# Gate rows of a two-layer streaming encoder: from weighted row sums to row sums of turned weights with a round trip through DRAM, and seven raw buffers in place of four

## The chip, the core and the metric

The kernel runs on one core of one Trainium2 chip. The metric is the device time of one execution in microseconds (us). TensorE is called PE, VectorE DVE, ScalarE ACT, GpSimd POOL, and SyncE SP; SP here only issues transfers (DMAs).

## What is computed

There are 256 tokens of 2048 features and two layers. In each layer a conditioning vector `c` gives six vectors of 2048 numbers (shift, scale and gate for the mixers, and the same three for the feed-forward part). This is the part that the change touches:

```python
c_act = jax.nn.silu(c)
for l in range(DEPTH):
    mod = (c_act @ w_mod[l] + b_mod[l]).reshape(bn, 6, d)
    ...
    h = layer_norm(x) * (1.0 + scale_m) + shift_m
    proj = h @ w_in[l]
    ...            # four groups of mixers, 512 columns each, give y
    y = jnp.concatenate([y_a, y_b, y_c, y_d], axis=-1) @ w_out[l]
    x = layer_norm(ALPHA * x + (1.0 + gate_m) * y, post_mix_g[l], post_mix_b[l])
    h = layer_norm(x) * (1.0 + scale_f) + shift_f
    y = conv_ffn(h, ffn_w_up[l], ffn_w_conv[l], ffn_b_conv[l], ffn_w_down[l])
    x = layer_norm(ALPHA * x + (1.0 + gate_f) * y, post_ffn_g[l], post_ffn_b[l])
```

All data are float32. `w_mod` is the largest part: 2048 x 12288 numbers in each layer, so 16 MB for each of the six vectors.

## The kernel before

**Products.** Weights come from DRAM in pieces of 1 MB into a buffer of the pool `rawp` (128 partitions x 2048 floats, four buffers; `weights`, line 368). ACT copies a piece into a rounded half `whi` (line 397), DVE takes the difference `wlo` (line 398), and PE multiplies `whi` and `wlo` with the two halves of the activations (`mm`, line 94). Both halves live in `splitp`, four buffers each. Where activations or weights are taken exactly (the first pieces of layer 0, the six first units of the second half of its output projection, the first group behind each norm), weights go straight into `splitp` or `slotp` buffers as `wexact` (line 381), without ACT and DVE.

**Order of the parts.** Layer 0 takes its mixers by pieces (`by_pieces`, line 1181), because its first shift and scale are themselves still being computed: units of modulation, conv block D and side groups U, V, E, B follow a list of turns. Then come group C, the attention, the output projection `out_proj` (line 603, tile `o`), the FFN up (tiles `g_c`, `v_c`), the FFN down (`out_proj` again, tile `d`), and layer 1 in the same way with whole groups. `out_proj` makes the 2048 output columns in two halves. When the last unit of the first half is reached it asks for the gate (line 762), and `finish_bank` multiplies each result bank with it (line 641, tile `yg`). Six PSUM buffers hold the results; a half takes four.

**Modulation.** It runs beside the products, on DVE. `mod_stream` (line 290) lists its parts, and `pump` takes some steps of it for each unit of weights, at rates written by hand for each phase (`RATES`, line 35). `need` (line 320) takes the steps that are missing when a vector is asked for. Each step loads 1 MB of `w_mod` into a raw buffer, so modulation and weights share the four buffers. Shift and scale are wanted as columns (one number for each partition): the weights lie turned in DRAM (`w_mod_turned`), and one instruction multiplies 128 rows of 2048 with `silu(c)` broadcast over the partitions (`cB`) and adds up each row (`row_sum`, line 191).

**Gates before.** A gate is wanted as a row that stands on all partitions. `gate_steps` (line 274) loads 16 pieces of `w_mod_gates` and adds them, each times one column of `silu(c)`, to `macc` (128 x 2048, a buffer of its own; `mod_step`, line 222). After the 16th the bias row is loaded into a raw buffer (`brow`, line 283) and added on partition 0 (line 286). The sum is then put into the list `late`. `settle` runs `gate_rows` (line 230) on it: the sum is split into halves `mhi` and `mlo` (lines 417 and 418, in `splitp` buffers), eight products with a matrix of ones sum over the partitions and spread the result (`ps_gate`), and four ACT copies add 1 and write the row `gate` (line 239). `settle` is called two steps into the next part, at the start of the next gate, or by `need`; for the last gate (layer 1, FFN) no part follows, so `need` calls it.

**Who orders the instructions.** The framework (Tile) fixes each engine's order when the program is built: it walks the program with a model of the engines, gives buffers out as they come free, and lets a free engine take the earliest written instruction whose inputs and buffers are there. So an instruction that is written late can be issued early where its engine has nothing older to do. SP and POOL issue their DMAs in that order, and an issue that waits for its buffer holds what stands behind it. A few order edges are written by hand (`held`, line 351: eight splits and six modulation steps wait for a norm).

POOL issues the small parameter loads (`load_params`, line 178) and makes the reciprocal roots of the norms (`power`, line 124).

Of the kernel before, what the change touches and what calls it, by code (L numbers as in the profile page):

```python
# [7 lines left out]
F32 = mybir.dt.float32  # L8
F32R = mybir.dt.float32r
AF = mybir.ActivationFunctionType  # L10
ALU = mybir.AluOpType
AX = mybir.AxisListType

P = 128
D = 2048
S = 256
DEPTH = 2
W_G = 512
KT = D // P
# [12 lines left out]
SHIFT_M, SCALE_M, GATE_M, SHIFT_F, SCALE_F, GATE_F = range(6)  # L32
# [16 lines left out]
LATE_KT = 12  # L49
# [2 lines left out]

LEAD, UNIT_LEAD = 2, 4

PAIRS = ((SHIFT_M, SCALE_M), (SHIFT_F, SCALE_F))

GROUPS = {
    "w_in": ((C_UV, 512), (C_UV + 512, 512), (C_Q, 768), (C_SB, 512), (C_SC, 1024), (C_AG, 1024)),
    "w_out": ((0, 1024), (1024, 1024)),
# [6 lines left out]
def encoder_kernel(ctx: ExitStack, tc: tile.TileContext, A: dict, consts: bass.AP, out: bass.AP):  # L66
    nc = tc.nc
    pe, act, dve, pool = nc.tensor, nc.scalar, nc.vector, nc.gpsimd

    keep = ctx.enter_context(tc.tile_pool(name="keep", bufs=1))  # L70
    rawp = ctx.enter_context(tc.tile_pool(name="rawp", bufs=4))
    splitp = ctx.enter_context(tc.tile_pool(name="splitp", bufs=4))
    tmpp = ctx.enter_context(tc.tile_pool(name="tmpp", bufs=4))
    actp = ctx.enter_context(tc.tile_pool(name="actp", bufs=10))
    slotp = ctx.enter_context(tc.tile_pool(name="slotp", bufs=11))
    smallp = ctx.enter_context(tc.tile_pool(name="smallp", bufs=2))
    accp = ctx.enter_context(tc.tile_pool(name="accp", bufs=6, space=bass.MemoryType.PSUM))
    msp = ctx.enter_context(tc.tile_pool(name="msp", bufs=2, space=bass.MemoryType.PSUM))


    def raw_tile(name):
        return rawp.tile([P, 2048], F32, tag="raw", name=name)

    def tmp_tile(name):
        return tmpp.tile([P, 512], F32, tag="tmp", name=name)

    def ms_tile(name):
        return msp.tile([P, 512], F32, tag="ms", name=name)
# [4 lines left out]
    def mm(o, lhsT, rhs, start, stop):  # L93
        pe.matmul(o, lhsT, rhs, start=start, stop=stop, skip_group_check=True)  # L94

    def ident_act(o, i, scale, bias):
        return act.activation(out=o, in_=i, func=AF.Identity, scale=scale, bias=bias)
# [7 lines left out]
    ident = cst[:, 0:128]  # L105
# [2 lines left out]
    rotdup = cst[0:64, 384:512]  # L108
    cosT = cst[:, 512:768]
    sinT = cst[:, 768:1024]  # L110
    flat = tmp_tile("flat")
    pool.memset(flat[:, 0:P], 1.0)
    pool.memset(flat[:, P : P + 16], 0.0)
    for j in range(4):
        pool.memset(flat[:, P + 5 * j : P + 5 * j + 1], 1.0)
    onesR = keep.tile([P, P + 16], F32R, name="onesR")
    act.copy(onesR, flat[:, : P + 16])
    ones = onesR[:, 0:P].bitcast(F32)
    mhalf = keep.tile([P, 4], F32, name="mhalf")
    pool.memset(mhalf, -0.5)  # L120
    eps = keep.tile([P, 1], F32, name="eps")
# [23 lines left out]
    bcol = []  # L145
# [3 lines left out]
    pool.dma_start(out=bcol[0], in_=A["b_mod_cols"][0])  # L149

    def scales_up(l):
        b = bcol[l].rearrange("p (h m) -> p h m", h=2)[:, :, KT : 2 * KT]
        dve.tensor_scalar(out=b, in0=b, scalar1=1.0, scalar2=None, op0=ALU.add)

    scales_up(0)
# [40 lines left out]

    def mod_unit(l, m, kt, total):
        raw = raw_tile("wmod")
        pair = PAIRS.index((m, m + 1)) if m in (SHIFT_M, SHIFT_F) else PAIRS.index((m - 1, m))
        nc.sync.dma_start(out=raw, in_=A["w_mod_turned"][l, 2 * pair + m % 3, kt])  # L200
        row_sum(raw, D, 0, total)

    def mod_done(l, m, k0, n, total):
# [9 lines left out]
                MOD[(l, m + h, k0 + k)] = cols[:, h, k : k + 1]  # L213
        return i

    def halves(acc, c0, width=1024):
        hi = splitp.tile([P, 1024], F32R, tag="whi", name="mhi")[:, :width]
        lo = splitp.tile([P, 1024], F32R, tag="wlo", name="mlo")[:, :width]
        split((hi, lo), acc[:, c0 : c0 + width])
        return [(hi[:, i : i + 512], lo[:, i : i + 512]) for i in range(0, width, 512)]  # L220

    def mod_step(acc, w, kt, first):
        col = cact[:, kt : kt + 1]
        if first:
            i = dve.tensor_scalar(out=acc, in0=w, scalar1=col, scalar2=None, op0=ALU.mult)
        else:
            i = dve.scalar_tensor_tensor(out=acc, in0=w, scalar=col, in1=acc, op0=ALU.mult, op1=ALU.add)  # L227
        held(i, "mod")

    def gate_rows(l, m, acc):  # L230

        g = keep.tile([P, D], F32, tag="gate", name=f"gate_{l}_{m}")
        for h in range(2):
            for i, (hi, lo) in enumerate(halves(acc, h * 1024)):
                c0 = h * 1024 + i * 512
                ps = ms_tile("ps_gate")
                mm(ps, onesR[:, 0:P], hi, True, False)
                mm(ps, onesR[:, 0:P], lo, False, True)
                ident_act(g[:, c0 : c0 + 512], ps, 1.0, ones[:, 0:1])
        GATE[(l, m)] = g  # L240

    GATE = {}
# [7 lines left out]
    def load_late_first():  # L250
        for m in (SHIFT_F, SCALE_F):
            for h in range(2):
                half = slot("wlate")
                nc.sync.dma_start(out=half, in_=A["w_mod_turned"][0, 2 + m % 3, LATE_KT, :, h * 1024 : (h + 1) * 1024])
                late_first[(m, h)] = half

    def columns(l, m, k0, k1):
# [16 lines left out]
    def gate_steps(l, m):  # L274
        while late:
            settle()
        acc = tmpp.tile([P, D], F32, tag="macc", name="macc", bufs=1)
        for kt in range(KT):
            raw = raw_tile("wmod")
            nc.sync.dma_start(out=raw, in_=A["w_mod_gates"][l, m // 3, kt])  # L280
            if kt == KT - 1:
                row = raw_tile("brow")
                nc.sync.dma_start(out=row[0:1, :], in_=A["b_mod"][l : l + 1, m * D : (m + 1) * D])
            mod_step(acc, raw, kt, kt == 0)
            if kt == KT - 1:
                dve.tensor_tensor(out=acc[0:1, :], in0=acc[0:1, :], in1=row[0:1, :], op=ALU.add)
                late.append((l, m, acc))
            yield

    def mod_stream():  # L290
# [60 lines left out]
    def held(i, kind):  # L351

        name, n = hold[kind]
        if n > 0:
            hold[kind][1] = n - 1
            tc.add_manual_dep(i.ins, name, order_dep, reason="the norm is what the next products wait for")
# [58 lines left out]
    def split(dst, src):  # L415
        hi, lo = dst[:2]
        i = act.copy(hi, src)
        dve.tensor_tensor(out=lo, in0=src, in1=hi.bitcast(F32), op=ALU.subtract)
        return i
# [1104 lines left out]


_INS = [
    "x", "b_mod", "gmlp_ln_g", "gmlp_ln_b", "gmlp_b_s", "mla_w_ukv", "post_mix_g", "post_mix_b",
    "post_ffn_g", "post_ffn_b",
]

# [1 line left out]
def _laid_out(inputs):  # L1532

    import numpy as np

    get = lambda name: np.asarray(inputs[name])
    cols = lambda name: get(name).reshape(DEPTH, -1, P).transpose(0, 2, 1)
    arrays = {name: get(name) for name in _INS}
    for name, groups in GROUPS.items():
        w = get(name)  # L1540
        for c0, width in groups:
            per = 2048 // width
            part = w[:, :, c0 : c0 + width].reshape(DEPTH, -1, per, P, width)
            arrays[f"{name}_{c0}_{width}"] = part.transpose(0, 1, 3, 2, 4)
    w = get("w_mod").reshape(DEPTH, D, 2, 3, KT, P)
    arrays["w_mod_turned"] = w[:, :, :, :2].transpose(0, 2, 3, 4, 5, 1).reshape(DEPTH, 4, KT, P, D)
    arrays["w_mod_gates"] = w[:, :, :, 2].transpose(0, 2, 1, 3, 4).reshape(DEPTH, 2, KT, P, D)
    arrays["c_cols"] = get("c").reshape(KT, P).T
    arrays["b_mod_cols"] = cols("b_mod")
    arrays["mixer_cols"] = np.concatenate(  # L1550
        [
            cols(name)
            for name in ("conf_w_dw", "mla_q_norm", "mla_kv_norm", "sconv_w", "conf_b_dw", "conf_ln_g", "conf_ln_b")
        ],
        axis=2,
    )
    arrays["ffn_cols"] = np.concatenate([cols("ffn_w_conv"), cols("ffn_b_conv")], axis=2)
    arrays["gmlp_w_turned"] = get("gmlp_w_s").transpose(0, 3, 1, 2).reshape(DEPTH, P, -1)
    uq = get("mla_w_uq").reshape(DEPTH, 3, P, HEADS, 192)
    arrays["mla_w_uq"] = np.concatenate(  # L1560
        [uq[..., :128].reshape(DEPTH, 3, P, -1), uq[..., 128:].reshape(DEPTH, 3, P, -1)], axis=3
    )
    return {name: np.ascontiguousarray(a) for name, a in arrays.items()}
# [28 lines left out]
def build(inputs):  # L1592
    import numpy as np
    import concourse.bacc as bacc

    nc = bacc.Bacc("TRN2", target_bir_lowering=False, num_devices=1)
    arrays, A = {}, {}
    for name, a in _laid_out(inputs).items():
        arrays[f"in_{name}_dram"] = a
        A[name] = nc.dram_tensor(f"in_{name}_dram", a.shape, mybir.dt.from_np(a.dtype), kind="ExternalInput").ap()  # L1600
    c = _constants()
    arrays["in_consts_dram"] = c
    consts = nc.dram_tensor("in_consts_dram", c.shape, F32, kind="ExternalInput").ap()
    out = nc.dram_tensor("out_0_dram", (1, S, D), F32, kind="ExternalOutput").ap()
    with tile.TileContext(nc) as tc:
        encoder_kernel(tc, A, consts, out)
    return nc, arrays
# [8 lines left out]
```

## Time and profile before

| what | value |
|---|---|
| median of 3 runs | 2243.66 us (2242.68 to 2244.53) |
| the profiled execution's own time | 2246.46 us |
| its span (first to last instruction) | 2244.7 us |
| mean granted clock of PE | 0.991 |
| data moved by DMA | 605.17 MB |

The profile shows one execution. A page gives the busy time of each engine, the chain of work that ended last, and the costliest groups of instructions; other views give the waits, the instructions in order of time, one tile's instructions, or a table by stretches of time. "Idle before, releaser" says how long an engine waited and for whom. Matmuls overlap: a busy PE is not yet a PE at its peak, and the distance from the start of one matmul to that of the next is what it costs.

### The profile page before, as it was taken

To read this page: it belongs to the slowest core of one execution; us is meant where nothing else is said; L and a number is where in the kernel's file an instruction comes from. 1 tells how busy PE (TensorE), PEld (TensorE's weight loads), DVE (VectorE), ACT (ScalarE), POOL (GpSimd) and SP (SyncE) were. 2 spreads that over 40 slices of the span, in tenths; PEclk is the share of its full clock that TensorE was granted. 3 is DMA by queue.
4 is the path that set the end of the run, shared out by engine and by line. 5 is a ranking of instruction groups with operands and counts; after the bars stand their busy time and mean duration, and the time that the engine had idled before them with its cause. 6 is when DMAs were issued, how large, how long until landed. Compare 5 with 4: busy or idle time off the path is not lost.

```text
span 2244.7 us, 30821 instructions
## 1 busy us (share of the span) xinstructions
PE 2200.6 (98%) x12128; PEld 1901.5 (85%) x12128; DVE 1738.9 (77%) x2222; ACT 1067.3 (48%) x1579; POOL 29.6 (1%) x49
## 2 busy tenths in 40 slices
PE   7999999999999999999999999999999999999997
PEld 5788885898888888888889899888888888888886
DVE  6778986988888888989876998977775656575756
ACT  3457541454455445544444435445444544454542
POOL 0000000000000000000000000000000000000000
PEclk9999999999999999999999999999999999999999
DMA  9999689688888888888867666865665555555553
GB/s 390 350 390 386 239 340 359 247 308 315 313 316 308 329 318 320 328 330 322 336 219 263 209 232 252 305 224 208 245 224 192 184 199 179 203 189 188 187 194 144
DMA packets 94235, 605.17 MB, mean 270 GB/s; under 512 B 10660, under 2 KB 10852, under 8 KB 28932
## 3 DMA queue, kind: packets, MB, share of 16 engines
q1 hardware_dynamic: 93752, 602.29, 71.8%
q8 instruction: 95, 1.56, 0.3%
q0 software_dynamic: 336, 0.89, 0.1%
q14 instruction: 52, 0.43, 0.1%
HBM read 601.05 MB, written 2.10 MB: 269 GB/s over the span
## 4 chain that ended last, share of the span: by engine, by line
PE 80%; DVE 4%; DMA 1%; ACT 1%; issue 1%; POOL 0%; DVEq 0%; ACTq 0%; POOLq 0%
PE g_c L94 23%; PE v_c L94 22%; PE d L94 21%; PE o L94 5%; PE C_c L94 2%; PE D_c L94 2%; PE U_c L94 1%; PE B_c L94 1%; PE E_c L94 1%; DVE wlo L398 1%; DMA wraw<-in_w_out_dram 1%; DVE convD L827 1%; PE ps_xT L534 0%; DVE wmod L192 0%; DMA wmod<-in_w_mod_turned_dram 0%
## 5 line engine op out<-in xcount | busy, mean ns | idle before, releaser
L397 ACT CAST whi<-wraw 128x1024 fp32r<-128x1024 f32 (+1 forms) x632 | 647.9, 1045 | 873.2 <-PE g_c L94 208.1
L398 DVE TENSOR_TENSOR wlo<-wraw,whi 128x1024 fp32r<-128x1024 f32 (+1 forms) x632 | 752.9, 1214 | 307.6 <-ACT whi L397 290.0
L94 PE MATMUL d<-whi,a 128*128 128x512 f32 x1344 | 364.1, 389 | 0.0
L94 PE MATMUL v_c<-hT,whi 128*128 128x512 f32 (+1 forms) x1456 | 341.8, 383 | 0.0
L94 PE MATMUL g_c<-hT,whi 128*128 128x512 f32 (+1 forms) x1344 | 313.3, 380 | 0.0
L192 DVE SCALAR_TENSOR_TENSOR wmod<-wmod,cB 128x2048 f32<-128x2048 f32 x126 | 287.4, 2286 | 31.9 <-DMA wmod<-in_w_mod_turned_dram 31.6
L94 PEld LDWEIGHTS v_c<-hT,whi 128*128 128x128 f32 x1456 | 264.5, 189 | 48.2 <-DVE g L1388 0.3
L94 PEld LDWEIGHTS d<-whi,a 128*128 128x128 f32 x1344 | 252.2, 188 | 52.5 <-ACT whi L397 0.2
L94 PEld LDWEIGHTS g_c<-hT,whi 128*128 128x128 f32 x1344 | 243.4, 189 | 43.2
L94 PE MATMUL d<-wlo,a 128*128 128x512 f32 x672 | 209.9, 389 | 0.0
L94 PE MATMUL v_c<-hT,wlo 128*128 128x256 f32 x1400 | 190.2, 283 | 0.0
L94 PEld LDWEIGHTS v_c<-hT,wlo 128*128 128x128 f32 x1400 | 183.1, 191 | 6.5
L94 PE MATMUL g_c<-hT,wlo 128*128 128x256 f32 x1280 | 175.8, 283 | 0.0
L94 PEld LDWEIGHTS g_c<-hT,wlo 128*128 128x128 f32 x1280 | 168.2, 191 | 5.9
L227 DVE SCALAR_TENSOR_TENSOR macc<-wmod,cact,macc 128x2048 f32<-128x2048 f32 x60 | 140.7, 2345 | 17.3 <-DMA wmod<-in_w_mod_gates_dram 17.2
L94 PEld LDWEIGHTS d<-wlo,a 128*128 128x128 f32 x672 | 126.2, 188 | 26.2
L94 PE MATMUL o<-whi,a 128*128 128x512 f32 x384 | 109.7, 395 | 2.4 <-ACT whi L397 2.4
L94 PEld LDWEIGHTS o<-whi,a 128*128 128x128 f32 x384 | 71.8, 188 | 20.1 <-ACT whi L397 4.1
L94 PE MATMUL D_c<-hT,whi 128*128 128x256 f32 x432 | 81.6, 292 | 1.7 <-ACT whi L397 1.7
L1337 DVE SCALAR_TENSOR_TENSOR u<-g,pf,u 128x254 f32<-128x254 f32 (+1 forms) x176 | 73.3, 476 | 0.0
L94 PEld LDWEIGHTS D_c<-hT,whi 128*128 128x128 f32 x432 | 68.8, 197 | 4.4 <-ACT whi L397 2.8
L94 PE MATMUL o<-wlo,a 128*128 128x512 f32 x192 | 63.0, 397 | 0.6 <-DVE wlo L398 0.5
(343 smaller groups left out, 2505.4 us busy)
## 6 DMA issues: line engine op xcount, KB each, us to landing
wraw<-in_ffn_w_up_dram SPq DMA_DIRECT2D x168, 1024.0 KB, 4.9
wmod<-in_w_mod_turned_dram SPq DMA_DIRECT2D x126, 1024.0 KB, 6.3
wraw<-in_ffn_w_down_dram SPq DMA_DIRECT2D x88, 1024.0 KB, 4.8
wmod<-in_w_mod_gates_dram SPq DMA_DIRECT2D x64, 1024.0 KB, 5.0
wraw<-in_w_in_dram SPq DMA_DIRECT2D x27, 1024.0 KB, 5.5
wraw<-in_w_out_dram SPq DMA_DIRECT2D x26, 1024.0 KB, 5.8
wexact<-in_w_in_dram SPq DMA_DIRECT2D x46, 512.0 KB, 9.6
wexact<-in_ffn_w_up_dram SPq DMA_DIRECT2D x16, 512.0 KB, 9.5
```

The source lines that it names most:

```text
L94: pe.matmul(o, lhsT, rhs, start=start, stop=stop, skip_group_check=True)
L192: i = dve.scalar_tensor_tensor(out=raw, in0=raw, scalar=1.0, in1=cB[:, k0 : k0 + n], op0=ALU.mult, op1=ALU.mult, accum_out=total)
L227: i = dve.scalar_tensor_tensor(out=acc, in0=w, scalar=col, in1=acc, op0=ALU.mult, op1=ALU.add)
L397: cast[0] = act.copy(hi[:, :m], r)
L398: i = dve.tensor_tensor(out=lo[:, :m], in0=r, in1=hi[:, :m].bitcast(F32), op=ALU.subtract)
L827: dve.scalar_tensor_tensor(out=yd[:, j, 30 - k :], in0=glu[:, j, : S - 30 + k], scalar=CW(k, j), in1=yd[:, j, 30 - k :], op0=ALU.mult, op1 ...
L1337: dve.scalar_tensor_tensor(out=u[:, sh:], in0=x[:, : S - sh], scalar=col(k, j), in1=u[:, sh:], op0=ALU.mult, op1=ALU.add)
```

## The change

The gates are now computed like shift and scale. `gate_steps` takes 16 row sums of turned weights into `total` (128 x 16), adds the bias columns (to which `scales_up` now adds the 1 as well), and puts the 128 x 16 result into `late`. `gate_rows` turns it with one PE transposition, copies the 16 x 128 result out of PSUM on ACT, writes it to DRAM as a row of 2048 (a POOL DMA of 8 KB), and loads that row back onto all 128 partitions (a second POOL DMA of 1 MB, which waits for the first). `macc`, `brow`, the splits, the eight products and the four copies go. The weights of all six vectors lie in `w_mod_turned`. The matrix of ones is set by one DVE instruction where POOL and ACT made it before.

The raw pool has seven buffers of 8 KB per partition where it had four. The space comes from `macc` (8 KB) and from the descriptor space of POOL's DMAs, which is set to 2048 bytes per partition (16384 when nothing is said).

```diff
-    rawp = ctx.enter_context(tc.tile_pool(name="rawp", bufs=4))
+    rawp = ctx.enter_context(tc.tile_pool(name="rawp", bufs=7))
...
+    dramp = ctx.enter_context(tc.tile_pool(name="dramp", bufs=1, space=bass.MemoryType.DRAM))
...
-    flat = tmp_tile("flat")
-    pool.memset(flat[:, 0:P], 1.0)
...
-    onesR = keep.tile([P, P + 16], F32R, name="onesR")
-    act.copy(onesR, flat[:, : P + 16])
-    ones = onesR[:, 0:P].bitcast(F32)
+    onesR = keep.tile([P, P], F32R, name="onesR")
+    dve.memset(onesR.bitcast(F32), 1.0)
+    ones = onesR.bitcast(F32)
...
-        b = bcol[l].rearrange("p (h m) -> p h m", h=2)[:, :, KT : 2 * KT]
+        b = bcol[l].rearrange("p (h m) -> p h m", h=2)[:, :, KT : 3 * KT]
...
-        pair = PAIRS.index((m, m + 1)) if m in (SHIFT_M, SHIFT_F) else PAIRS.index((m - 1, m))
-        nc.sync.dma_start(out=raw, in_=A["w_mod_turned"][l, 2 * pair + m % 3, kt])
+        nc.sync.dma_start(out=raw, in_=A["w_mod_turned"][l, m, kt])
         row_sum(raw, D, 0, total)
...
-    def gate_rows(l, m, acc):
-
+    def gate_rows(l, m, cols):
+
+        ps = ms_tile("ps_gate")
+        pe.transpose(ps[0:KT, 0:P], cols, ident)
+        rows = tmp_tile("grows")[0:KT, 0:P]
+        act.copy(rows, ps[0:KT, 0:P])
+        flat = dramp.tile([KT, P], F32, tag=f"gate{l}{m}", name=f"gate_row_{l}_{m}")
+        pool.dma_start(out=flat, in_=rows)
         g = keep.tile([P, D], F32, tag="gate", name=f"gate_{l}_{m}")
-        for h in range(2):
-            for i, (hi, lo) in enumerate(halves(acc, h * 1024)):
-                c0 = h * 1024 + i * 512
-                ps = ms_tile("ps_gate")
-                mm(ps, onesR[:, 0:P], hi, True, False)
-                mm(ps, onesR[:, 0:P], lo, False, True)
-                ident_act(g[:, c0 : c0 + 512], ps, 1.0, ones[:, 0:1])
+        pool.dma_start(out=g, in_=flat.rearrange("k j -> (k j)").partition_broadcast(P))
         GATE[(l, m)] = g
...
-        acc = tmpp.tile([P, D], F32, tag="macc", name="macc", bufs=1)
+        total = smallp.tile([P, KT], F32, tag="gtotal", name="gtotal", bufs=1)
         for kt in range(KT):
-            raw = raw_tile("wmod")
-            nc.sync.dma_start(out=raw, in_=A["w_mod_gates"][l, m // 3, kt])
+            mod_unit(l, m, kt, total[:, kt : kt + 1])
             if kt == KT - 1:
-                row = raw_tile("brow")
-                nc.sync.dma_start(out=row[0:1, :], in_=A["b_mod"][l : l + 1, m * D : (m + 1) * D])
-            mod_step(acc, raw, kt, kt == 0)
-            if kt == KT - 1:
-                dve.tensor_tensor(out=acc[0:1, :], in0=acc[0:1, :], in1=row[0:1, :], op=ALU.add)
-                late.append((l, m, acc))
+                cols = smallp.tile([P, KT], F32, tag="gcols", name="gcols", bufs=1)
+                dve.tensor_tensor(out=cols, in0=total, in1=bcol[l][:, m * KT : (m + 1) * KT], op=ALU.add)
+                late.append((l, m, cols))
             yield
...
-    nc = bacc.Bacc("TRN2", target_bir_lowering=False, num_devices=1)
+    nc = bacc.Bacc("TRN2", target_bir_lowering=False, num_devices=1, dynamic_dma_scratch_size=2048)
```

More of the change, by code (lines that the diff above doesn't have):

```diff
@@ L53 @@
 LEAD, UNIT_LEAD = 2, 4
-PAIRS = ((SHIFT_M, SCALE_M), (SHIFT_F, SCALE_F))
 GROUPS = {
@@ L110, in encoder_kernel @@
     sinT = cst[:, 768:1024]
-    flat = tmp_tile("flat")
-    pool.memset(flat[:, 0:P], 1.0)
-    pool.memset(flat[:, P : P + 16], 0.0)
-    for j in range(4):
-        pool.memset(flat[:, P + 5 * j : P + 5 * j + 1], 1.0)
-    onesR = keep.tile([P, P + 16], F32R, name="onesR")
-    act.copy(onesR, flat[:, : P + 16])
-    ones = onesR[:, 0:P].bitcast(F32)
+    onesR = keep.tile([P, P], F32R, name="onesR")
+    dve.memset(onesR.bitcast(F32), 1.0)
+    ones = onesR.bitcast(F32)
     mhalf = keep.tile([P, 4], F32, name="mhalf")
@@ L214, in mod_done @@
         return i
[L216 to L228, printed above, removed]
-    def gate_rows(l, m, acc):
-        g = keep.tile([P, D], F32, tag="gate", name=f"gate_{l}_{m}")
-        for h in range(2):
-            for i, (hi, lo) in enumerate(halves(acc, h * 1024)):
-                c0 = h * 1024 + i * 512
-                ps = ms_tile("ps_gate")
-                mm(ps, onesR[:, 0:P], hi, True, False)
-                mm(ps, onesR[:, 0:P], lo, False, True)
-                ident_act(g[:, c0 : c0 + 512], ps, 1.0, ones[:, 0:1])
+    def gate_rows(l, m, cols):
[5 more added lines that the diff above has]
+        pool.dma_start(out=flat, in_=rows)
+        g = keep.tile([P, D], F32, tag="gate", name=f"gate_{l}_{m}")
+        pool.dma_start(out=g, in_=flat.rearrange("k j -> (k j)").partition_broadcast(P))
         GATE[(l, m)] = g
@@ L253, in load_late_first @@
                 half = slot("wlate")
-                nc.sync.dma_start(out=half, in_=A["w_mod_turned"][0, 2 + m % 3, LATE_KT, :, h * 1024 : (h + 1) * 1024])
+                nc.sync.dma_start(out=half, in_=A["w_mod_turned"][0, m, LATE_KT, :, h * 1024 : (h + 1) * 1024])
                 late_first[(m, h)] = half
@@ L1526 @@
 _INS = [
-    "x", "b_mod", "gmlp_ln_g", "gmlp_ln_b", "gmlp_b_s", "mla_w_ukv", "post_mix_g", "post_mix_b",
+    "x", "gmlp_ln_g", "gmlp_ln_b", "gmlp_b_s", "mla_w_ukv", "post_mix_g", "post_mix_b",
     "post_ffn_g", "post_ffn_b",
@@ L1544, in _laid_out @@
             arrays[f"{name}_{c0}_{width}"] = part.transpose(0, 1, 3, 2, 4)
-    w = get("w_mod").reshape(DEPTH, D, 2, 3, KT, P)
-    arrays["w_mod_turned"] = w[:, :, :, :2].transpose(0, 2, 3, 4, 5, 1).reshape(DEPTH, 4, KT, P, D)
-    arrays["w_mod_gates"] = w[:, :, :, 2].transpose(0, 2, 1, 3, 4).reshape(DEPTH, 2, KT, P, D)
+    w = get("w_mod").reshape(DEPTH, D, 6, KT, P)
+    arrays["w_mod_turned"] = w.transpose(0, 2, 3, 4, 1)
     arrays["c_cols"] = get("c").reshape(KT, P).T
```

## The prediction

> **What bounds the kernel now.** I read the head of the page first, then the chain of work that ended last in order of time, and then the busy times by stretches. On the page:
>
> ```profile
> span 2244.7 us, 30821 instructions
> ...
> PE 2200.6 (98%) x12128; PEld 1901.5 (85%) x12128; DVE 1738.9 (77%) x2222; ACT 1067.3 (48%) x1579; POOL 29.6 (1%) x49
> ...
> PE 80%; DVE 4%; DMA 1%; ACT 1%; issue 1%; POOL 0%; DVEq 0%; ACTq 0%; POOLq 0%
> ```
>
> PE is busy nearly all the time and makes 80% of the chain. So an edit pays in two ways only: it takes work off PE where PE runs without a break, or it shortens one of the places where PE waits. The table by stretches (columns: length, then PE, PEld, DVE, ACT, POOL busy with counts, PE clock, DMA share, GB/s) tells which stretch is which. First the three that hold the gates 2 to 4 (layer 0 FFN, layer 1 mixer, layer 1 FFN):
>
> ```profile
> 600.00:650.00 50.00, 50.00 (x288) 43.86 (x288) 43.29 (x53) 28.58 (x44) 0.00 (x0) 1.00 0.83 322
> ...
> 1350.00:1400.00 50.00, 49.99 (x398) 48.91 (x396) 44.44 (x57) 26.41 (x34) 0.00 (x0) 1.00 0.67 244
> ...
> 2100.00:2150.00 50.00, 50.00 (x221) 40.90 (x220) 36.42 (x41) 26.98 (x33) 0.00 (x0) 1.00 0.51 180
> ```
>
> PE has no break in them, at full clock, while DVE and DMA have room: here a matmul less is time less. Then layer 0's mixer, in which gate 1 lies, in finer steps:
>
> ```profile
> 10.00:20.00 10.00, 4.16 (x13) 1.91 (x11) 8.68 (x17) 5.70 (x11) 3.15 (x2) 0.75 1.02 419
> ...
> 50.00:60.00 10.00, 10.00 (x44) 7.47 (x43) 2.10 (x6) 4.46 (x8) 0.00 (x0) 1.00 0.72 291
> 60.00:70.00 10.00, 9.76 (x64) 8.58 (x63) 8.94 (x10) 6.59 (x13) 0.00 (x0) 1.00 0.81 304
> 70.00:80.00 10.00, 7.86 (x43) 6.67 (x43) 9.39 (x14) 3.86 (x8) 0.00 (x0) 0.99 0.91 338
> 80.00:90.00 10.00, 9.26 (x50) 9.07 (x51) 7.80 (x10) 2.84 (x5) 0.00 (x0) 0.67 1.00 362
> ...
> 260.00:270.00 10.00, 10.00 (x50) 8.81 (x49) 9.24 (x14) 2.13 (x5) 0.00 (x0) 1.00 0.29 107
> ...
> 310.00:320.00 10.00, 10.00 (x45) 8.21 (x45) 10.00 (x11) 4.38 (x7) 0.00 (x0) 1.00 0.77 307
> ...
> 330.00:340.00 10.00, 9.14 (x37) 6.27 (x36) 7.95 (x8) 4.00 (x4) 0.00 (x0) 1.00 1.01 384
> 340.00:350.00 10.00, 8.09 (x35) 6.05 (x34) 9.47 (x9) 1.99 (x2) 0.00 (x0) 1.00 0.99 363
> ```
>
> PE waits at 70 to 90 and at 330 to 350, and after the first wait its clock falls to 0.67 for ten microseconds. Yet DMA, which reaches 419 GB/s, ran at 291 and 304 just before the first wait, and at 107 some way before the second. What stops it is told by SP's own waits over the first 420 us, and what PE waited for by the instructions around 77 us:
>
> ```profile
> SPq L200 <- DVE wlo L398: 57.9, 17, 13.7
> SPq L386 <- DVE wmod L192: 41.6, 14, 9.8
> ```
>
> ```profile
> 77.47 1.04 ACT L397 CAST whi<-wraw 128x1024 fp32r<-128x1024 f32 x1 [3.44 <-DMA wraw<-in_w_in_dram]
> ...
> 78.56 0.97 PE L94 MATMUL D_c<-hT,whi 128*128 128x256 f32 x6 [1.69 <-ACT whi L397]
> ```
>
> Modulation loads (L200) wait until a weight piece is split, and weight loads (L386) until a modulation piece is summed: the two take turns in four buffers, 99.5 us of waiting in these two rows alone. When the buffer comes, the piece lands late, ACT waits 3.44 us for it and PE 1.69 us for ACT.
>
> **The change, part by part. 1: gate products off PE.** The chain around gate 2 (start, length, what):
>
> ```profile
> 602.14 22.27 PE g_c L94 x128
> 624.87 0.68 PE v_c L94 x3
> 626.21 1.37 PE v_c L94 x6
> 628.27 0.70 PE ps_gate L94 x3
> 628.98 19.75 PE v_c L94 x117
> 648.72 22.27 PE g_c L94 x128
> ...
> 1389.98 0.93 PE ps_gate L94 x4
> ...
> 1496.47 3.57 PE g_c L94 x32
> ```
>
> A group of 128 matmuls takes 22.27 us. The group that holds the gate starts at 602.14 + 22.27 = 624.41 and ends at 648.72, 24.31 us: the gate costs 2.04 us (its eight matmuls at 0.70 / 3 = 0.23 us are 1.87 of them). In its place comes one transposition, 128 columns wide. The last row is 32 exact matmuls of that width, 0.11 us each. So a gate gives 1.93 us, and the three in stretches without a break give **5.8 us**. Gate 1's products also go, 1.87 - 0.11 = **1.8 us**, but PE waits 60 us later, at 330 to 350: this counts only if those waits shrink too, so I count it with the buffers.
>
> **2: DVE and ACT.** Work around one gate, by tile (ns min/median/max):
>
> ```profile
> L227 DVE SCALAR_TENSOR_TENSOR macc<-wmod,cact,macc x60: 2322/2346/2353, 162.7 to 1648.3; 128x2048 f32<-128x2048 f32 x60
> ...
> L192 DVE SCALAR_TENSOR_TENSOR wmod<-wmod,cB x126: 2270/2284/2295, 13.7 to 1108.6; 128x2048 f32<-128x2048 f32 x126
> ...
> L286 DVE TENSOR_TENSOR macc<-macc,brow x4: 2266/2272/2273, 253.3 to 1653.8; 1x2048 f32<-1x2048 f32 x4
> ...
> L418 DVE TENSOR_TENSOR mlo<-macc,mhi x8: 1215/1224/1226, 261.9 to 2112.1; 128x1024 fp32r<-128x1024 f32 x8
> ```
>
> The 16 steps cost about the same before and after (2.35 against 2.28 us). The bias on one partition (2.27) and two splits (2 x 1.22) go: some 4.7 us of DVE for each gate, against one small addition. For gates 2 to 4 this is worth nothing: PE, which has no break there, hides it; without that cover it would be at most the 4.7. At gate 1 DVE is 92% busy (9.24 of 10 in the row 260 to 270) and the 4.7 us help the waits of part 3, in whose price I leave them.
>
> **3: seven raw buffers.** PE's loss in the rows above: 2.14 + 0.74 idle at 70 to 90, 9.26 x 0.33 = 3.06 for the low clock behind it, 0.86 + 1.91 idle at 330 to 350; together 8.7 us. Three more buffers are 3 MB, 7.5 us of transfer at 419 GB/s, which may start earlier. Ahead of 70 to 90 DMA has 2.8 + 1.9 + 0.9 = 5.6 us free, enough to cover the 5.1 us that ACT and PE waited; of 5.9 us lost I take 4.0, since DMA has no room left from 80 on and part of the wait may come again a little later. At 330 to 350 DVE is in the way as well (10.00 of 10 at 310 to 320), and of the 2.8 us I take 1.0. Sum **5.0 us**, bounds 0 and 8.7; below nothing is the third rival. The first norm of layer 0 may also win, or lose, one or two steps of modulation that stand in its chain:
>
> ```profile
> 394.91 2.21 DVE wmod L192 x2
> ```
>
> that is 2.2 us either way; I take nothing. Where PE has no break the buffers bring nothing.
>
> [...]
>
> **4: the round trip.** Transposition, ACT copy, 8 KB to DRAM, 1 MB back. The nearest rows (DMA issues: line, count, KB, median us to landing), the planner's POOL order, the last gate's times and the first use of the third:
>
> ```profile
> gb<-in_post_mix_g_dram SPq DMA_DIRECT2D x2, 1024.0 KB, 13.9
> ...
> gb<-in_post_ffn_g_dram SPq DMA_DIRECT2D x2, 1024.0 KB, 5.4
> ...
> out_dram<-x SPq DMA_DIRECT2D x8, 256.0 KB, 2.3
> ```
>
> ```profile
> 2.21 0.54 POOL L183 DMA_DIRECT2D bcol<-in_b_mod_cols_dram  x1
> ```
>
> ```profile
> 2109.66 1.05 ACT L417 CAST mhi<-macc 128x1024 fp32r<-128x1024 f32 x1 [2.51 <-PE d L94]
> ...
> 2114.39 1.28 DVE L641 TENSOR_TENSOR yg<-d,gate 128x512 f32<-128x512 f32 x2
> ```
>
> ```profile
> 1442.49 1.29 DVE L641 TENSOR_TENSOR yg<-o,gate 128x512 f32<-128x512 f32 x2 [0.18 <-PE o L94]
> ```
>
> A store lands in 2.3 us, a row spread over all partitions in 5.4 to 13.9, two POOL issues cost 2 x 0.54, transposition and copy perhaps 0.5 (an estimate from the widths above): 9.3 to 17.8 us. [...] Of gates 1 to 3 the third has the least time: made at 1389.98 and first used at 1442.49, 52 us later, so nobody waits. On POOL's queue the second DMA waits for the first, and the roots of the norms stand behind it; the next is tens of microseconds off. The four spread loads add 4 MB; gate 1's finds DMA 29% busy at 260, the others lie under PE.
>
> The last gate is written by `need` where it is used. Before, its work began at 2109.66 and `yg` at 2114.39, so 4.7 us are covered; a trip of 9.3 to 17.8 us would leave 4.6 to 13.1 us in which DVE stands at `yg`, with the splits of the next weights behind it, and PE waiting for splits and for result banks. But its columns are ready 450 us earlier, and unlike `mhi` the transposition needs no split buffer. Line 183's load, written behind the first output projection, is at 2.21 us in POOL's order: the planner pulls ready work forward. I take **0**, and keep about 5 us (the near end) as a case.
>
> **5: the rest.** The ones from one DVE instruction, the weights' layout, the small descriptor space: nothing here waits for them, 0.
>
> Sum: 5.8 + 1.8 + 5.0 = 12.6 us. On the profiled execution's own 2246.5 us this gives 2233.9; that execution is 2.8 us over the median, so the forecast for the median 2243.7 is **2231**.
>
> **The rivals.** *Buffers bring nothing:* DVE or the DMA rate sets the pace of layer 0, waits only move, and gate 1's 1.8 us drown in them. For it: DVE full at 310, DMA share 1.00 at 80. Against: the free DMA at 50 to 70 and at 260. Time: 2243.7 - 5.8 = 2238. The same time results if the planner doesn't use the buffers. [...]
>
> *The last round trip is exposed:* 5 us back at 2115. With the buffers' gain 2236, without it 2243.
>
> *Modulation runs ahead of weights (slower):* three more buffers let three more 1 MB modulation loads stand before the weights in SP's one queue, where DMA has no room (from 80 us on). The weights come 3 x 2.5 = 7.5 us later, PE stands once, and its clock falls as at 80 to 90 (3.1 us): 7.5 + 3.1 - 5.8 = 4.8 us slower, 2248.5. It decides where a weight piece lands later than the two turns that it is loaded ahead. For it: both kinds share the queue. Against: the weights are written first in each turn, and today it is they who wait for modulation to give up buffers. [...]
>
> *More than forecast:* all of the 8.7 us, 2.2 at the norm, smaller waits: about 2223.
>
> **How the numbers follow.** What a measurement of this kernel can tell is 0.2%, 4.5 us: below 2239.2 is faster, above 2248.1 slower. Chances: forecast 0.50 (its own range 2226 to 2236), buffers nothing 0.20, exposed 0.10, slower 0.08, more 0.12. Faster takes the forecast, the larger gain, most of the second case and half of the exposed one: 0.78. Same 0.13, slower 0.09. The range from 2220 to 2243 leaves out the slower case and the far ends.
>
> **What would show it.** Right: eight `ps_gate` products per gate gone and the group at 624 back near 22.4 us; PE nearly unbroken at 70 to 90 with its clock up; fewer and shorter SP waits before 420; the transposition of gate 4 long before 2100. Wrong: DMA unchanged at 50 to 70 (second case); `yg` near 2115 waiting for a POOL DMA; PE waiting longer at 80 to 130 behind `wraw` while `wmod` loads stand ahead of it in SP's order.

## The result and the profile after

The changed kernel takes 2231.43 us (median of 4 runs, 2231.06 to 2232.02), the kernel before in the same session 2243.86 (4 runs, 2242.68 to 2244.53): 12.4 us less, ratio 0.994 (95% interval 0.9928 to 0.9952). The forecast was 2231. The sum came out; two of its terms did not, and they nearly cancel. Most of what follows is about that.

The head of the page of the kernel after:

```profile
span 2229.7 us, 30799 instructions
...
PE 2185.8 (98%) x12100; PEld 1893.4 (85%) x12100; DVE 1722.5 (77%) x2279; ACT 1052.3 (47%) x1557; POOL 34.5 (2%) x51
...
PE 88%; DVE 7%; issue 2%; ACT 2%; DMA 1%; POOL 0%; DVEq 0%; SPq 0%; POOLq 0%; ACTq 0%
```

PE has 28 instructions less (32 products out, 4 transpositions in) and 14.8 us less of busy time; DVE and ACT lost 16 and 15 us. The profiled execution took 2231.45 us, 15.0 less than the profiled one before; the medians differ by 12.4. Of the profiled executions the furthest lies 2.7 us from its kernel's median (2244.28 against 2241.60, the kernel with the unused products below), so stage figures from two profiles are good to that, and totals are taken from medians.

The chain around gate 2, to be held against the one in the prediction (start, length, what):

```profile
592.60 22.26 PE g_c L93 x128
614.87 0.11 PE ps_gate L212
614.98 14.75 PE v_c L93 x80
...
629.75 7.65 DMA wmod<-in_w_mod_turned_dram
...
637.49 2.30 DVE wmod L186 x2
639.79 0.35 DVE second L1370
...
640.18 20.72 PE g_c L93 x120
```

The gate is now one piece of 0.11 us, as reckoned; but behind it stands a chain that was not there before, from a modulation load over DVE to PE. The timeline tells the idle times in it and whom each engine waited for:

```profile
637.49 2.29 DVE L186 SCALAR_TENSOR_TENSOR wmod<-wmod,cB 128x2048 f32<-128x2048 f32 x1 [3.23 <-DMA wmod<-in_w_mod_turned_dram]
...
640.18 2.11 PE L93 MATMUL g_c<-hT,whi 128*128 128x512 f32 x8 [1.07 <-DVE second L1370]
```

DVE stands 3.23 us at a modulation piece whose load went out at 629.75 and took 7.65 us; behind it in DVE's order stands an instruction (`second`, line 1370) that frees PE's result bank, and PE waits 1.07 us.

The same stretches as before, where PE had waited (length, then PE, PEld, DVE, ACT, POOL busy with counts, PE clock, DMA share, GB/s):

```profile
70.00:80.00 10.00, 8.48 (x51) 7.53 (x49) 9.43 (x12) 4.35 (x8) 0.00 (x0) 1.00 0.99 363
80.00:90.00 10.00, 8.35 (x50) 8.15 (x51) 8.90 (x13) 4.20 (x7) 0.00 (x0) 0.83 0.99 382
330.00:340.00 10.00, 9.43 (x42) 7.46 (x41) 9.97 (x10) 1.86 (x2) 0.00 (x0) 1.00 0.60 224
340.00:350.00 10.00, 10.00 (x31) 5.46 (x30) 10.00 (x15) 0.00 (x0) 0.00 (x0) 1.00 1.00 374
```

At 330 to 350 PE's idle time fell from 2.77 to 0.57 us and DVE is now the full engine. At 70 to 90 the wait is still there (3.17 us idle, against 2.88), with a clock that falls less. Yet the free DMA ahead of it is used, where 291 and 304 GB/s ran before:

```profile
50.00:60.00 10.00, 10.00 (x45) 7.86 (x44) 1.66 (x5) 3.55 (x7) 0.00 (x0) 1.00 1.02 416
60.00:70.00 10.00, 9.76 (x60) 8.21 (x59) 8.44 (x10) 6.61 (x12) 0.00 (x0) 1.00 1.01 410
```

The wait has another releaser now. Before, PE waited 1.69 us for ACT behind a late weight piece, and then 1.20 us for DVE; now it waits 3.17 us for DVE's split, and on the chain two row sums of modulation stand ahead of that split:

```profile
75.39 4.43 DVE wmod L186 x4
...
80.38 1.23 DVE wlo L373
...
81.65 6.80 PE D_c L93 x42
```

SP's longest waits over the first 420 us:

```profile
SPq L193 <- DVE wlo L373: 44.6, 11, 10.8
...
SPq L361 <- DVE wmod L186: 16.7, 7, 4.3
```

The two rows that were 57.9 and 41.6 (lines 200 and 386 before) are 44.6 and 16.7: weights wait for modulation less than half as long.

Where the time came from is read by taking the same matmul of both traces and subtracting its start. The table does so for four kernels (negative: earlier than before; the kernels of the last three columns are described below):

| matmul, start before (us) | after | four buffers | six buffers, old gates | settled early |
|---|---|---|---|---|
| first chunk of D done, 47.0 | +0.9 | +1.3 | -1.1 | +1.1 |
| last of group E, 173.8 | -3.8 | -0.6 | -5.7 | -5.1 |
| first of `o`, 303.4 (gate 1 lies before it) | -5.4 | -2.2 | -5.7 | -5.0 |
| first of `g_c`, 410.8 (behind the first norm) | -10.6 | -1.6 | -9.9 | -10.3 |
| `g_c` at 571.2 | -9.4 | -1.6 | -8.7 | -8.9 |
| `g_c` at 693.8 (behind gate 2) | -10.1 | -3.7 | -8.9 | -9.5 |
| `U_c` at 1175.9 (layer 1 begins) | -12.0 | -5.5 | -5.5 | -11.4 |
| first of `E_c`, 1372.5 | -13.0 | -4.3 | -5.9 | -12.4 |
| `o` at 1423.5 (behind gate 3) | -14.2 | -6.4 | -5.9 | -13.7 |
| `g_c` at 1552.7 | -15.1 | -7.1 | -6.6 | -14.3 |
| last of `d`, 2232.6 (behind gate 4) | -15.2 | -7.2 | -6.7 | -16.5 |

Read the column "after" by its steps: the start loses 0.9; layer 0 then gains 4.7 to the end of group E, 1.5 over gate 1 and 5.3 up to the FFN, and gives 1.3 back; gate 2 brings 0.7, the norm before layer 1 some 1.9, the mixers of layer 1 1.0, gate 3 1.2, the stretch behind it 0.9, gate 4 0.1.

The 1.3 given back lie in one wait. ACT makes a split (`whi`, 1.05 us) and four parts of `hF` ahead of the next products:

```profile
462.62 7.14 PE L93 MATMUL g_c<-hF,wexact 128*128 128x256 f32 x32 [1.77 <-ACT hF L96]
```

The kernels below with five to seven buffers have this wait too (1.40 to 1.77 us), the two with four buffers do not.

The 1.9 at the norm before layer 1 are mostly clock. Before, PE waits 1.46 us there in two pieces, and the granted clock behind them is down (0.92 over 1150 to 1160, 0.81 over 1160 to 1165: some 1.8 us lost); after, it waits 1.20 us and keeps the full clock.

The end of that list is in the timeline around the last gate (start, length, what, and idle time before it with its releaser):

```profile
2090.33 0.27 PE L212 MATMUL ps_gate<-cst,gcols 128*16 128x128 f32 x1
...
2092.03 0.54 POOL L216 DMA_DIRECT2D gate_row<-grows  x1 [604.72 <-ACT grows L214]
...
2094.21 0.56 POOL L218 DMA_DIRECT2D gate<-gate_row  x1 [1.64 <-DMA gate_row<-grows]
...
2101.14 1.29 DVE L616 TENSOR_TENSOR yg<-d,gate 128x512 f32<-128x512 f32 x2 [2.10 <-DMA gate<-gate_row]
...
2101.89 0.50 PE L93 MATMUL d<-whi,a 128*128 128x512 f32 x1 [1.72 <-DVE yg L616]
```

The transposition was not made early. The round trip takes 10.8 us from 2090.33 to `yg`, DVE stands at `yg` for 2.1 us, and PE waits 1.72 us for a result bank.

And the start, before and after. Before:

```profile
4.90 2.49 DVE L160 TENSOR_TENSOR diag<-cst,cact 128x512 f32<-128x512 f32 x4
5.64 3.78 PE L94 MATMUL ps_c<-diag,onesR 128*128 128x512 f32 x4 [5.64 <-DVE diag L160]
...
7.79 0.18 DVE L153 TENSOR_SCALAR bcol<-bcol 128x32 f32<-128x32 f32 x1 [0.39 <-DMA bcol<-in_b_mod_cols_dram]
```

After:

```profile
4.80 0.20 DVE L147 TENSOR_SCALAR bcol<-bcol 128x64 f32<-128x64 f32 x1 [3.80 <-DMA bcol<-in_b_mod_cols_dram]
7.82 0.20 DVE L147 TENSOR_SCALAR bcol<-bcol 128x64 f32<-128x64 f32 x1 [2.83 <-DMA bcol<-in_b_mod_cols_dram]
7.93 1.29 DVE L154 TENSOR_TENSOR diag<-cst,cact 128x512 f32<-128x512 f32 x2
...
8.67 1.22 PE L93 MATMUL ps_c<-diag,onesR 128*128 128x512 f32 x1 [8.67 <-DVE diag L154]
```

In DVE's order the addition of 1 to the second layer's bias columns now stands ahead of the diagonals, and it waits 2.83 us for a load. So the first products begin at 8.67 in place of 5.64.

### The profile page after: what moved, and what is told of

It reads as the page before. It is cut to its first block, busy times and chain, and to the rows that moved or that the text cites. A ratio compares the mean times of both kernels' runs of the same rounds, so it can differ in the third digit from the quotient of the medians.

```text
span 2229.7 us, 30799 instructions
## 1 busy us (share of the span) xinstructions
PE 2185.8 (98%) x12100; PEld 1893.4 (85%) x12100; DVE 1722.5 (77%) x2279; ACT 1052.3 (47%) x1557; POOL 34.5 (2%) x51
## 4 chain that ended last, share of the span: by engine, by line
PE 88%; DVE 7%; issue 2%; ACT 2%; DMA 1%; POOL 0%; DVEq 0%; SPq 0%; POOLq 0%; ACTq 0%
PE g_c L93 23%; PE v_c L93 22%; PE d L93 21%; PE o L93 6%; PE C_c L93 4%; PE D_c L93 4%; DVE wmod L186 2%; PE U_c L93 1%; DVE wlo L373 1%; PE U L93 1%; PE B_c L93 1%; PE E L93 1%; PE E_c L93 1%; PE V L93 1%; DVE convD L824 1%
## 5 line engine op out<-in xcount | busy, mean ns | idle before, releaser
L186 DVE SCALAR_TENSOR_TENSOR wmod<-wmod,cB 128x2048 f32<-128x2048 f32 x190 | 433.1, 2286 | 33.5 <-DMA wmod<-in_w_mod_turned_dram 32.7
L93 PEld LDWEIGHTS g_c<-hT,whi 128*128 128x128 f32 x1344 | 243.4, 189 | 44.6 <-DVE second L1370 1.5
L93 PE MATMUL g_c<-hF,wexact 128*128 128x128 f32 (+1 forms) x480 | 61.1, 288 | 2.8 <-ACT hF L96 2.7
L93 PE MATMUL D_c<-hT,wlo 128*128 128x256 f32 x216 | 60.4, 288 | 3.2 <-DVE wlo L373 3.2
```

The source lines that it names most:

```text
L186: i = dve.scalar_tensor_tensor(out=raw, in0=raw, scalar=1.0, in1=cB[:, k0 : k0 + n], op0=ALU.mult, op1=ALU.mult, accum_out=total)
```

## Experiments

My theory after the result: the buffers bring more than was counted, the gates less, because the last round trip is exposed and the new order costs something at the start and behind gate 2. The rival: the gates bring their 7.6 us as counted, and the buffers the rest. The runs come from three sessions, in which the kernel before had medians of 2243.86, 2244.56 and 2244.73 us, so a difference from the changed kernel, which was timed in the first, is good to about 1 us at best.

**The gates without the buffers.**

```diff
-    rawp = ctx.enter_context(tc.tile_pool(name="rawp", bufs=7))
+    rawp = ctx.enter_context(tc.tile_pool(name="rawp", bufs=4))
```

> The changed kernel with four raw buffers instead of seven: the gates alone. Theory (most of the gain is the buffers' in layer 0; gates 1 to 3 give up to 1.9 us each, the last gate's gain is eaten by its round trip): 2238 to 2242 us, and PE waits near 75 and near 335 us as before. Rival (the buffers bring nothing, the time comes from the gates' lighter work on DVE and ACT and from a new order): 2231 to 2234.

Measured: 2241.12 us (11 runs, 2239.07 to 2244.83) against 2244.56 (18 runs), ratio 0.9987 (0.9979 to 0.9996): the gates alone bring 3.4 us. In the table, gates 2 and 3 bring 2.1 and 2.1, as the removed products cost, and gate 4 nothing. (The two executions that the table compares lie 7.4 us apart, more than the medians: this kernel's is the fastest of its eleven, and the one before is slower than its median.) PE, which had no break there before (50.00 of 50 us), now has one (the stretch around the last gate):

```profile
2075.00:2125.00 50.00, 48.47 (x214) 39.71 (x213) 34.17 (x39) 23.80 (x28) 1.10 (x2) 1.00 0.57 210
```

The rival falls: 3.4 (by the interval 0.9 to 4.7) is not 7.6, and some 9 us are left to the buffers.

**The buffers without the gates.** The kernel before, with six buffers (its `macc` stays) and a smaller descriptor space:

```diff
-    rawp = ctx.enter_context(tc.tile_pool(name="rawp", bufs=4))
+    rawp = ctx.enter_context(tc.tile_pool(name="rawp", bufs=6))
...
-    nc = bacc.Bacc("TRN2", target_bir_lowering=False, num_devices=1)
+    nc = bacc.Bacc("TRN2", target_bir_lowering=False, num_devices=1, dynamic_dma_scratch_size=1024)
```

> The kernel before with six raw buffers instead of four (descriptor space 1024 bytes), the gates as they were: two of the three added buffers alone. Theory: the waits near 75 and 335 us shrink, 2234 to 2238. Rival (buffers bring nothing): 2242 to 2245.

Measured: 2238.04 us (7 runs, 2234.11 to 2242.85), ratio 0.9972 (0.996 to 0.9984), 6.5 us less. Layer 0's mixer and first norm gain 9.9 us, nearly as much as in the changed kernel, and 3.3 are given back at the norm before layer 1 (-8.9 to -5.5 in the table). Where PE waited at 325 to 350, first with four buffers and the new gates, then with six and the old:

```profile
325.00:350.00 25.00, 22.98 (x91) 17.80 (x90) 22.78 (x25) 6.00 (x6) 0.00 (x0) 0.93 1.00 394
```

```profile
325.00:350.00 25.00, 23.76 (x91) 16.65 (x90) 24.97 (x28) 3.65 (x4) 0.00 (x0) 1.00 0.95 373
```

With four buffers PE idles 2.0 us and its clock is down to 0.93; with six 1.2, at full clock, and DVE is busy throughout. With four buffers and the old gates it was 2.8, with seven and the new 0.6: that wait goes by the buffers with either kind of gate.

The 3.3 given back are a late load and the clock behind it: PE waits for the exact weights of layer 1's first group, and the granted clock is at half behind the start of that wait (0.50 over 1150 to 1156). These 32 matmuls take 5.79 us, where 32 of the same shape take 3.74 in the trace before (from 1496.30, at full clock).

```profile
1152.24 5.79 PE L94 MATMUL U_c<-hF,wexact 128*128 128x128 f32 x32 [4.18 <-DMA wexact<-in_w_in_dram]
```

**The round trip made early.** The waiting gate is settled as soon as the list of modulation parts has ended, and not when `need` asks (two lines at the end of `mod_stream`):

```diff
+        while late:
+            settle()
```

> The changed kernel with the last gate settled right after its last step and not where it is used. Theory (the round trip is exposed at the last gate): PE's wait of 1.7 us near 2100 goes, 1.5 to 2 us faster than the changed kernel, 2229.5. Rival (the wait there is for PSUM banks whatever the gate does): no difference, 2231.4.

Measured: 2229.97 us (5 runs, 2229.23 to 2230.58), ratio 0.9934 (0.9922 to 0.9946), some 1.5 us under the changed kernel. The intervals of the two overlap, so the trace has to show the gain. The transposition now comes 425 us earlier, the spread load follows it at once, and PE has no break around the last gate:

```profile
1665.07 0.27 PE L212 MATMUL ps_gate<-cst,gcols 128*16 128x128 f32 x1
...
1668.59 0.56 POOL L218 DMA_DIRECT2D gate<-gate_row  x1 [1.64 <-DMA gate_row<-grows]
```

```profile
2075.00:2125.00 50.00, 50.00 (x223) 41.39 (x222) 35.41 (x40) 24.61 (x28) 0.00 (x0) 1.00 0.57 198
```

From 2087 to 2137 this trace gains 2.2 us on the one of the changed kernel, so that the last gate now saves about what its products had cost. The planner did not move the step; writing it earlier did.

**The diagonals first.** An order edge (no wait on data) puts the second layer's bias behind the last diagonal:

```diff
-        dve.tensor_scalar(out=b, in0=b, scalar1=1.0, scalar2=None, op0=ALU.add)
+        return dve.tensor_scalar(out=b, in0=b, scalar1=1.0, scalar2=None, op0=ALU.add)
...
-        dve.tensor_tensor(
+        last_diag = dve.tensor_tensor(
...
-            scales_up(l)
+            i = scales_up(l)
+            tc.add_manual_dep(i.ins, last_diag.ins.name, order_dep, reason="the first products wait for the diagonals")
```

> The changed kernel with an order edge at the start: the diagonals for the broadcast of silu(c) stand before the second layer's bias columns on DVE. Theory (the first product on the data waits 1.9 us longer than before because DVE stands for the bias load): the first D product at 19 to 20 us as before, 0.5 to 2 us faster in all. Rival (the weight loads set the pace by 60 us anyway): no difference.

Measured: 2230.02 us (5 runs, 2228.13 to 2230.62), ratio 0.9933 (0.9921 to 0.9945), some 1.4 us less, again with overlapping intervals. The start is back, and at 47 us this kernel is 2.1 us ahead of the changed one:

```profile
5.05 2.49 DVE L154 TENSOR_TENSOR diag<-cst,cact 128x512 f32<-128x512 f32 x4
5.79 3.78 PE L93 MATMUL ps_c<-diag,onesR 128*128 128x512 f32 x4 [5.79 <-DVE diag L154]
```

The PE wait behind gate 2 is gone in this kernel too, as it is with four buffers: it belongs to the order that the planner happened on, and the new gate can do without it.

**The products put back, for nobody.** Eight products of ones by ones in each gate; their result is not used:

```diff
+        dummy = ms_tile("ps_dummy").rearrange("p (k j) -> p k j", k=4)
+        for n in range(8):
+            mm(dummy, onesR, onesR.unsqueeze(1).to_broadcast([P, 4, P]), n == 0, n == 7)
```

> The changed kernel with eight products of 128x512 of the ones by themselves put into each gate (result unused): PE gets back the work that the change took from it. Theory (PE has no break where gates 2 to 4 lie): 1.8 us for each of gates 2 to 4 and up to 1.8 for gate 1, so 5.4 to 7.3 us slower than the changed kernel, 2237 to 2239. Rival (these products were hidden behind waits): 2231 to 2233.

Measured: 2241.60 us (11 runs, 2238.54 to 2246.32) against 2244.73 (15 runs), ratio 0.9988 (0.998 to 0.9997): 10.2 us more than the changed kernel, where 5.4 to 7.3 had been expected (9.3 if each kernel is held against the one before in its own session). Gates 1 and 2 lose 1.9 us each where the products stand, of which 1.4 come back behind gate 2, where the wait is shorter; gate 4 loses 0.5 (its wait hides the rest). Gate 3 loses 6.9. There the order shifted so that PE came to wait for the square of a norm (`ps_var`); two-microsecond stretches behind it:

```profile
1390.00:1392.00 2.00, 0.40 (x4) 0.40 (x4) 1.55 (x6) 1.08 (x2) 0.00 (x0) 1.00 0.74 217
1392.00:1394.00 2.00, 2.00 (x15) 2.00 (x16) 1.23 (x1) 1.01 (x2) 0.00 (x0) 0.78 0.87 340
1394.00:1396.00 2.00, 2.00 (x12) 2.00 (x11) 0.00 (x0) 0.00 (x0) 0.00 (x0) 0.50 0.28 115
1396.00:1398.00 2.00, 2.00 (x11) 2.00 (x11) 0.35 (x2) 0.00 (x0) 0.71 (x1) 0.50 0.05 20
1398.00:1400.00 2.00, 2.00 (x8) 1.81 (x8) 1.58 (x4) 1.07 (x2) 0.00 (x0) 0.52 0.00 0
```

One idle of 2.12 us, and by these rows the clock is at half for some 6.8 us: 2.1 us of idle, 3.4 of lost clock and 1.9 for the products are together a little more than the 6.9. The price per gate of part 1 is confirmed where the products alone changed; the total is not a clean price, since any edit reorders the rest.

**Five buffers**, and five with the full descriptor space (the second part of the diff is in the second kernel alone):

```diff
-    rawp = ctx.enter_context(tc.tile_pool(name="rawp", bufs=7))
+    rawp = ctx.enter_context(tc.tile_pool(name="rawp", bufs=5))
...
-    nc = bacc.Bacc("TRN2", target_bir_lowering=False, num_devices=1, dynamic_dma_scratch_size=2048)
+    nc = bacc.Bacc("TRN2", target_bir_lowering=False, num_devices=1)
```

> The changed kernel with five raw buffers (four gave 2241.1, seven 2231.4). Theory (each buffer lets one more load run ahead, the first ones matter most): 2235 to 2238. Rival (only the seventh buffer or none matters): 2240 to 2242.

> The same with five raw buffers and the descriptor space of POOL's DMAs at its full 16384 bytes. Theory (the small space costs nothing, POOL makes few DMAs): the same time as with five buffers and 2048 bytes, within 1 us. Rival (a small space delays POOL's DMAs): 1 to 3 us faster than that.

Measured: 2234.52 us (5 runs, 2232.49 to 2238.47), ratio 0.9956 (0.9944 to 0.9969), and 2236.36 (5 runs, 2231.65 to 2238.72), ratio 0.9958 (0.9945 to 0.997). They were expected within 1 us and lie 1.8 apart, the fuller space being the slower; the intervals lie over one another, so the small descriptor space costs nothing that these runs can tell. The fifth buffer brings 6.6 us, the sixth and seventh 3.1 together, a difference at which the intervals still overlap.

**Both repairs.** The edits of the round trip and of the diagonals together:

> Both edits that won 1.4 us each (the last gate settled early, the diagonals first), with seven buffers. Theory (they lie 2000 us apart and add up): 2228 to 2229. Rival (a new order of the planner takes one of them back): 2230 to 2231.

Measured: 2227.25 us (5 runs, 2225.34 to 2229.12), ratio 0.9921 (0.9907 to 0.9934), some 4 us under the changed kernel and the fastest of all. That is a little better than the 2228 to 2229 of two gains that add up.

## Why the prediction was right, and where not

**1, gate products off PE: priced rightly, kept only in part.** The 1.93 us per gate are what the unbroken stretches showed: 2.1 at gates 2 and 3 with four buffers, 1.9 when the products were put back, 2.2 at the last gate once the round trip was out of the way. Of the 5.8 us for gates 2 to 4 the changed kernel has 0.7 + 1.2 + 0.1 = 2.0; gate 1, counted at 1.8, has about 1.5. At gate 2, 1.4 us are lost 25 us later, in the chain from the late modulation load to PE. Of gate 3's missing 0.7 a wait of 0.22 us for DVE (`dgD`) is a part; for the rest I have no cause.

**2, DVE and ACT: right.** DVE lost 16.4 us of work, 4 x 4.1, where 4.7 for each gate had been reckoned. Around gates 2 to 4 PE had no break that it could have shortened; what it gave at gate 1 is part of the buffers' gain and was not tried apart.

**3, buffers: right in kind, too small.** Counted 5.0, measured 9.7 between the medians of four and seven buffers (9.0 if each is held against the kernel before in its session, 8.0 between their profiles, and 6.5 in the old kernel with six). Seven buffers with the old gates were not run, so how the 12.4 divide depends on the order: 3.4 for gates that come first, or up to 5.9, with the seventh buffer in it, for gates that come after six buffers.

The first wait was put at 4.0, and 4.7 are gained up to the end of group E, though not as I reckoned: the idle at 70 to 90 is still there. The free DMA ahead of it was used, as expected, but DVE's row sums then held the split, and I had put no DVE into that term. (The 5.1 us set against the free DMA also added ACT's wait and PE's, which are one chain.) The gain comes in pieces of about 1 us between 72 and 168, one of them the clock at 80 to 90 (0.83 in place of 0.67). That clock is not the buffers': with four buffers and the new gates it did not fall there at all (1.00 over 80 to 90). Of these 4.7 the kernel with four buffers has 1.9 too, so at most part of it is the buffers'.

The term that was mis-sized most is the second: 1.0 for the wait at 330 to 350, and nothing for the norm behind it. Between 303 and 411 us the changed kernel gains 5.3 us, the one with six buffers and old gates 4.2, the one with four buffers none. I had held DVE to be in the way there, since it was full at 310. But at 330 to 350 it had stood 2.6 of 20 us; with pieces at hand it works through (9.97 and 10.00 of 10) and PE follows.

The case in which the buffers bring nothing let DVE or the DMA rate set the pace of layer 0. In the kernel before, the rate was not at its end there. The pages have it in 40 slices of 56 us, before and after:

```profile
GB/s 390 350 390 386 239 340 359 247 308 315 313 316 308 329 318 320 328 330 322 336 219 263 209 232 252 305 224 208 245 224 192 184 199 179 203 189 188 187 194 144
```

```profile
GB/s 390 392 386 411 259 350 358 316 323 313 332 308 317 318 330 305 343 329 322 318 221 231 228 270 258 283 224 215 257 207 190 182 196 188 190 189 194 205 195 87
```

The first four slices, layer 0's mixers in them, stand at 386 to 411 GB/s after, where they stood at 350 to 390, and the runs give the buffers 6.5 to 9.7 us.

**4, the round trip: this step failed.** I took 0 because the columns are ready 450 us early and the planner pulls ready work forward. By tile, first and last of four:

```profile
L261 DVE TENSOR_TENSOR gcols<-gtotal,bcol x4: 167/171/175, 250.2 to 1624.8; 128x16 f32<-128x16 f32 x4
...
L212 PE MATMUL ps_gate<-cst,gcols x4: 270/270/272, 273.4 to 2090.3; 128*16 128x128 f32 x4
```

They were ready at 1624.8, and the transposition was issued at 2090.3. What I drew on, line 183's load at 2.21 us, is a POOL instruction, and POOL is idle (1% busy). PE, which must make the transposition, has no gap in which the planner could put it (465.00 of 465 us busy from 1625 to 2090). A missing result buffer is not the reason, since nothing in the trace after uses the two buffers of that pool between 1504 and 2090. That the lack of a gap is the reason is argued, and fits all four gates (columns ready at 250, 569, 1345 and 1625, transpositions at 273, 615, 1366 and 2090, with PE busy for 22.77 of 23 us, 46.00 of 46 and 21.00 of 21 between the first three pairs); that writing it earlier moves it is shown. The case I had kept aside happened, at a smaller price: 10.8 us of round trip, DVE 2.1 us late, and PE 1.7, which with the gate's own saving makes nothing. The whole trip of 10.8 us lies in the 9.3 to 17.8 that the rows gave. The two transfers took 9.1 us of it, from 2092.03 to 2101.14.

**5, the rest at 0: failed at the start.** In the new order, with the ones on DVE and the wider bias scaling, the second layer's scaling came to stand ahead of the diagonals and waited for its load; the first products start 3.0 us later, of which 0.9 are left at 47 us. Putting the diagonals first gained 2.1 us there. Nothing waits for the value, but in DVE's order the diagonals stand behind it and wait too. Which of the edits made the planner choose this order was not tried apart; the buffers did not, for with four the start is late as well (1.3 at 47 us).

So the forecast was 12.6 = 7.6 + 5.0, and the runs have 12.4, near 3.4 for the gates, start and all, and some 9 for the buffers. The total was met by two errors of opposite sign, which is luck; the mechanisms of parts 1 and 3 were right in kind. *Buffers bring nothing* and *modulation ahead of weights* are out: weights wait less for modulation (41.6 to 16.7 us). The 1.07 us that PE waits behind gate 2 are the nearest to the second that is left, and there it is modulation that comes late. *The round trip exposed* did happen, for 2 us in place of 5.

What stays open: why the load before layer 1 came late with the old gates and six buffers, and how much of such a step is the planner's luck. The single edits move the order everywhere, and stages shift by 1 to 3 us with no direct cause.

## What to carry to other kernels

Here the planner pulled ready work forward on an idle engine (POOL, 1% busy) and not on the bound one (PE, 98%). Where a step on the bound engine happens where it is written, write a long-latency chain at the moment its inputs are known: here that moved the transposition 425 us forward and gained some 1.5 us. One instruction that waited for a load held what stood behind it in its engine's order, though its own result wasn't wanted for long: 2.83 us of waiting on DVE, and the first products began 3.03 us later. When an engine looks full, ask whether it is full of work or full by having waited before: at 330 to 350 DVE had stood 2.6 of 20 us, and the buffers paid far more than counted where it had seemed to be the limit (up to 5.3 us between 303 and 411, counted 1.0).

## What the runs showed of the hardware

- Behind a wait of 2.12 us on PE the granted clock was at half for some 6.8 us (the rows of the kernel with the unused products). In the kernel before it was 1.00 over 76 to 78, where a wait of 1.69 us begins (up to 78.56), 0.97 over 78 to 80 and 0.50 over 80 to 86, with a second wait of 1.20 us up to 80.74 inside. In the kernel after it stayed at 1.00 around the wait of 1.72 us at 2100 to 2102. The length of a single wait does not decide it in these traces: the kernel settled early waits 3.16 us at the same place as the changed one (3.17), and keeps the full clock where the other falls to 0.83:

```profile
81.87 0.39 PE L93 MATMUL D_c<-hT,wlo 128*128 128x256 f32 x1 [3.16 <-DVE wlo L375]
...
80.00:90.00 10.00, 8.13 (x56) 7.79 (x57) 8.87 (x15) 4.20 (x7) 0.00 (x0) 1.00 1.02 413
```

- In the kernel after, the four loads of one row onto all partitions, issued by POOL, landed after 4.9 to 9.6 us (median 8.2). Each depends on an 8 KB store and was issued 2.1 to 2.2 us after it at gates 2 to 4, of which 1.6 were waiting for the store to land; at gate 1 it was issued 5.7 us after it, and 5.1 were that wait. By tile:

```profile
L218 POOL DMA_DIRECT2D gate<-gate_row x4: 550/552/561, 280.0 to 2094.2; - x4
...
DMA to landing us min/median/max: 4.9/8.2/9.6
```
